# FFN1's norm weight multiplied into the input's blocks out of PSUM instead of into weight rows, and the first pair of each FFN written in another order

## The chip, the core and the metric

The kernel runs on one core of a Trainium2 chip. The metric is device microseconds of one execution, median of several runs. TensorE (PE in the profile) multiplies into PSUM, VectorE (DVE) and ScalarE (ACT) read PSUM and SBUF, GpSimd (POOL) does a few additions, and SyncE (SP) issues nearly all DMAs. Each engine takes its instructions strictly in the order in which they stand in its queue.

## What is computed

One layer with two feed-forward blocks (FFN1, FFN2) around a mixer, for 16 meta tokens, 1024 prompt tokens and 8 sample tokens, together T = 1048 columns. The change concerns the two FFNs. Cut to that:

```python
def rmsnorm(x, w):
    y = x * lax.rsqrt(jnp.mean(x * x, axis=-1, keepdims=True) + EPS)
    return y * w

def swiglu(x, wg, wu, wd):          # wg, wu: 1024 x 2816, wd: 2816 x 1024
    return (jax.nn.silu(x @ wg) * (x @ wu)) @ wd

h = h + 0.5 * swiglu(rmsnorm(h, n1), w1g, w1u, w1d)   # FFN1
...
h = h + 0.5 * swiglu(rmsnorm(h, n2), w2g, w2u, w2d)   # FFN2
```

The norm weight n1 scales the 1024 features of the input. It may be multiplied into the input or into the 1024 rows of wg and wu; the factor rsqrt(mean) of a token is applied later, to the products.

## The kernel before

**Staging.** The span begins with FFN1: 22 "pairs" (a gate and an up block of 128 columns each, `pair`), then its `down` product. The mixer follows, then FFN2 with the same 22 pairs and `down`. FFN1 reads x from memory, transposes it on PE and places it (`Input`, `first1`); FFN2 has its input on chip (`first2`).

**A pair.** The input is held as two halves of the columns, each half (c = 0, 1) as 2 x 2 blocks: features 0-511 or 512-1023 by two quarters of 262 columns. Gate and up weights of one pair are 2 x 2 blocks too (gate or up by feature half). A product of 2 x 2 by 2 x 2 blocks is made of seven block products instead of eight, so both sides need sums of blocks: `Left.sum_` (L368) makes the weights' sums, `Blocks.sum_` (L288) the input's. Every operand is split into a rounded high part (ACT, L372 for weights, L293 for the input) and the remainder (DVE, L376, L299), and a block product is 4 feature tiles by 3 matmuls (high by high, high by low, low by high; L143 to L145) of 128x262. With seven products and two halves, a pair is 14 steps of 12 matmuls. The input's operands are made once, in the first pair, and stay for all 22; the weights' are made for every pair.

**Norm weight.** In FFN1, `Left.scale` (L362) multiplies n1 into the four loaded weight tiles of a pair: 16 ACT instructions of 128x128 each, in place, ahead of the sums. In FFN2 there is no such step: the input's blocks are scaled once by `Blocks.scaled` (L282).

**What sets the order.** Both FFNs are written under a manual schedule for PE, DVE, ACT and SP: `Steps.before(i, fn)` puts fn's instructions ahead of step i, and each engine's queue follows the order in which the steps are run through. `Left.plan` gives a pair's loads, scales, sums and splits by their distance to its first step (loads 11 and 10 steps ahead, sums 7 to 5 ahead). `Hidden.jobs` puts differences of the pair's result (L542) and their stores (L545) around the pairs' ends. SP takes loads (L355) and stores in one queue. After a product, `post` takes it out of PSUM: L459 (ACT) copies product 1, L461, L466, L468, L471 and L475 (DVE) add, L454 multiplies the token factor, L464 and L473 (ACT) are the silus, L481 writes the result. Products 1 and 2, 5 and 3, 7 and 4 share a PSUM bank, so that a later product waits for the copy or the addition of the earlier one.

**First pairs.** In the first pair of each FFN the steps run half by half (here o is half 0, e is half 1), since the input arrives late. `first1` in FFN1: `Input.place` transposes x tile by tile (L843) and copies blocks out of PSUM (L849: half 0 on DVE, half 1 on ACT); `square` (L860) sums squares for the token factor; `rms` (L875) and `spread_r` (L881, L882) spread the factor over partitions; `store` (L866) writes the transposed x to memory, from where `down` reads it back. The parameters come in one tile and one transpose (`columns`, L742).

Of the kernel before, what the change touches and what calls it, by code (L numbers as in the profile page):

```python
# [262 lines left out]
class Blocks:  # L263

    def __init__(self, K, half, keep=False):
        self.K, self.half, self.keep = K, half, keep
        self.b, self.op = {}, {}
# [74 lines left out]
class Left:  # L344
# [11 lines left out]

    def scale(self, p):
        if self.wcol is not None:
            for k in range(self.n):
                c = k + (self.n if p in (4, 2) else 0)  # L360
                t = self.raw[p][:, k * P : k * P + P]
                self.K.nc.scalar.activation(t, t, AF.Identity, scale=self.wcol[:, c : c + 1])  # L362
# [73 lines left out]
def pair(K, S, wg, wu, f, ops, spread, wcol, hid, first=None):  # L436
# [8 lines left out]
    left = Left(K, [wg[:, 0:4, fs], wu[:, 0:4, fs], wu[:, 4:8, fs], wg[:, 4:8, fs]], 4, wcol)  # L445
# [239 lines left out]
def ffn(K, wg, wu, wd, ops, spread, wcol, src, first, after):  # L685
# [9 lines left out]
    with K.tc.manual_schedule(engines={E.PE, E.DVE, E.Activation, E.SP}):  # L695
        S = Steps()
        hidden = Hidden(K)
        for i in range(NF // 2):
            hid, e = [], []
            for f in (2 * i, 2 * i + 1):  # L700
                hid.append([])
                pair(K, S, wgv, wuv, f, ops, spread, wcol, hid[-1], first if f == 0 else None)
# [23 lines left out]
def parameters(K, a):  # L726

    nc = K.nc
    rows = {"norm_ffn1": 8, "norm_mix": 8, "norm_ffn2": 8, "conv_w": 32, "conv_b": 8, "hg_norm": 4, "ssm_norm": 4, "lb_logits": 8}
    off = {}  # L730
    n = 0
    prm = K.t(P)
    for name, r in rows.items():
        off[name] = (n, r)
        (nc.scalar if name == "norm_ffn1" else nc.gpsimd).dma_start(prm[n : n + r, :], a[name].rearrange("l (k p) -> (l k) p" if len(a[name].shape) == 2 else "l j (k p) -> (l j k) p", p=P))
        n += r
    K.col = K.const.tile([P, n], F32, name="col")
# [73 lines left out]
class Input:  # L811
# [23 lines left out]
    def place(self, i, copy):  # L835
# [4 lines left out]
        for b0 in range(0, KT, m):  # L840
            ps = K.psm()
            for k in range(m):
                K.nc.tensor.transpose(ps[:, k * n : k * n + n], self.x[i][:, (b0 + k) * P : (b0 + k + 1) * P], K.ident[:n, :n])  # L843
            pv = ps[:, : m * n].rearrange("p (k t) -> p k t", k=m)
            for q in range(4):
                c0, c1 = max(t0, q * Q), min(t0 + n, q * Q + Q)
                for b in range(b0 // 4, (b0 + m) // 4):
                    if c0 < c1:
                        copy(self.block(b, q)[:, :, c0 - q * Q : c1 - q * Q], pv[:, 4 * b - b0 : 4 * b - b0 + 4, c0 - t0 : c1 - t0])  # L849

    def block(self, b, q):
# [4 lines left out]
        return o.b[p].rearrange("p (k t) -> p k t", k=4)  # L856

# [614 lines left out]
def body(ctx, tc, a, o):  # L1472
# [3 lines left out]
    columns = parameters(K, a)  # L1476
    wn1, wnm, wn2 = K.pc["norm_ffn1"], K.pc["norm_mix"], K.pc["norm_ffn2"]
    hsp = K.dram.tile([D, T], F32, name="hspill")
    ops = [Blocks(K, 0, keep=True), Blocks(K, 1)]
    spread = Spread(K)  # L1480
    x = Input(K, a, ops, spread)

    def first1(S, w):
        o, e = ops
        dve, act = nc.vector.tensor_copy, nc.scalar.copy
# [7 lines left out]
        x.place(0, dve)  # L1493
        x.square(0)
        columns()
        x.place(1, dve)
        x.square(1)
        x.place(2, dve)
        w.scale(1)
        o.cast(1)  # L1500
        w.hi(1)
        o.low(1)
        x.place(3, dve)
        w.lo(1)
        x.place(4, dve)
        o.cast(2)
        w.scale(2)
        w.hi(2)
        o.low(2)
        w.lo(2)  # L1510
        o.sum_(5)
        o.cast(5)
        x.store(0)

        def before(i, *fns):
            for fn in fns:
                S.before(i, (lambda fn=fn: fn[0](*fn[1:])))

        before(1, (w.scale, 7), (w.scale, 4), (w.sum_, 5), (w.hi, 5), (o.low, 5), (w.lo, 5), (o.sum_, 6), (o.cast, 6), (x.place, 5, act), (x.square, 2))
        before(2, (w.sum_, 6), (w.hi, 6), (o.low, 6), (w.lo, 6), (o.sum_, 7), (o.cast, 7), (x.square, 3), (x.square, 4), (x.place, 6, act))  # L1520
# [217 lines left out]
```

## Time and profile before

| what | us |
|---|---|
| median of 3 runs (2224.08 to 2236.66) | 2226.96 |
| the profiled execution: its time, its span | 2225.85, 2224.1 |
| busy in the span: PE, DVE, ACT | 2044.1, 1495.2, 894.5 |
| FFN1's pairs: first gate load of pair 2 issued, that of pair 21 | 92.30, 543.48 |
| FFN2's pairs: the same two loads | 1524.86, 1916.19 |

How to read it: the page has busy times, the chain of work that ended last, and groups of instructions by line. A row of the timeline has start, duration, engine, line, operation, output and input, count, and in brackets the idle time of the engine ahead of it with what ended it. A row of waits has the engine and line that waited, what it waited for, the total in us, how often, and the longest. A row of windows has the stretch, its length, busy time of PE, PE's weight loads, DVE, ACT and POOL with counts, the granted TensorE clock, the DMA engines' busy share, and GB/s.

### The profile page before, as it was taken

How to read it: one execution, taken by the hardware profiler on the slowest of the kernel's cores; microseconds unless marked ns; L12 is line 12 of the kernel's file. 1: busy time of each engine (PE TensorE's matmuls, PEld its weight loads, DVE VectorE, ACT ScalarE, POOL GpSimd, SP SyncE). 2: the span in 40 equal slices, each digit the busy share in tenths (PEclk: the TensorE clock that was granted, in tenths of full speed). 3: DMA queues.
4: the chain of work that ended last, by engine and by line, in shares of the span. 5: the costliest groups of instructions: out<-in, count | busy, mean ns of one | idle time of the engine just before them, and what ended most of it. 6: DMA issues, size and time to landing. Idle time of an engine off the chain costs nothing.

```text
span 2224.1 us, 38759 instructions
## 1 busy us (share of the span) xinstructions
PE 2044.1 (92%) x15494; PEld 1983.2 (89%) x15494; DVE 1495.2 (67%) x2498; ACT 894.5 (40%) x1799; POOL 141.9 (6%) x175
## 2 busy tenths in 40 slices
PE   5698988998989989979999998979999999989996
PEld 4698988988989988978899997969999999989996
DVE  5666666666778767568554556576777777778863
ACT  5634434434334544365423325552222222333351
POOL 1000000000000210050110110220000000000000
PEclk8899999999999999989999999999999999999998
DMA  6133232233795551063220233322323323487651
GB/s 184 40 98 91 73 101 73 73 101 96 224 292 176 175 162 40 12 171 99 81 77 13 67 108 129 125 67 73 100 74 116 101 83 105 144 268 235 209 149 56
DMA packets 325036, 259.19 MB, mean 117 GB/s; under 512 B 17713, under 2 KB 301105, under 8 KB 324849
## 3 DMA queue, kind: packets, MB, share of 16 engines
q1 hardware_dynamic: 324616, 256.68, 38.5%
q8 instruction: 122, 2.00, 0.4%
q14 instruction: 58, 0.47, 0.1%
q0 software_dynamic: 224, 0.04, 0.0%
q10 hardware_dynamic: 16, 0.00, 0.0%
HBM read 191.26 MB, written 65.47 MB: 115 GB/s over the span
## 4 chain that ended last, share of the span: by engine, by line
PE 58%; DVE 16%; DMA 9%; ACT 7%; issue 4%; SPq 1%; POOL 1%; DVEq 0%; ACTq 0%; POOLq 0%
PE acc L143 18%; PE acc L144 17%; PE acc L145 17%; DMA r<-in_w_ffn_up_dram 5%; ACT r L362 4%; DVE t L454 2%; DVE ws L376 2%; DMA r<-in_w_ffn_down_dram 2%; PE mis L1328 1%; ACT ws L372 1%; DVE s L481 1%; DVE r L368 1%; DMA u<-hd 1%; DVE s L641 1%; DVE s L542 1%
## 5 line engine op out<-in xcount | busy, mean ns | idle before, releaser
L143 PE MATMUL acc<-u,ws 128*128 128x262 f32 (+2 forms) x4504 | 1337.3, 298 | 116.5 <-DVE t L466 53.2
L144 PE MATMUL acc<-u,ws 128*128 128x262 f32 (+2 forms) x4504 | 1326.5, 295 | 2.3 <-DVE u L299 1.2
L145 PE MATMUL acc<-u,ws 128*128 128x262 f32 (+2 forms) x4504 | 1323.9, 294 | 1.7 <-DVE ws L376 1.6
L143 PEld LDWEIGHTS acc<-u,ws 128*128 128x128 f32 x4504 | 867.5, 193 | 139.5 <-ACT r L362 46.0
L144 PEld LDWEIGHTS acc<-u,ws 128*128 128x128 f32 x4504 | 872.0, 194 | 4.6 <-DVE u L299 1.9
L145 PEld LDWEIGHTS acc<-u,ws 128*128 128x128 f32 x4504 | 868.6, 193 | 2.9 <-DVE ws L376 2.2
L376 DVE TENSOR_TENSOR ws<-r,ws 128x512 fp32r<-128x512 f32 x308 | 212.2, 689 | 162.9 <-ACT ws L372 162.9
L372 ACT CAST ws<-r 128x512 fp32r<-128x512 f32 x308 | 175.0, 613 | 5.9 <-PE acc L145 5.1
L362 ACT ACTIVATE r<-r,col 128x128 f32<-128x128 f32 x352 | 108.0, 388 | 119.5 <-DMA r<-in_w_ffn_up_dram 119.5
L368 DVE TENSOR_TENSOR r<-r,r 128x512 f32<-128x512 f32 x176 | 119.3, 697 | 29.2 <-ACT r L362 24.0
L473 ACT ACTIVATE t<-t 128x524 f32<-128x524 f32 (+1 forms) x46 | 28.7, 623 | 269.2 <-DVE t L454 269.2
L204 POOL TENSOR_TENSOR t<-t,t 128x262 f32<-128x262 f32 x56 | 52.0, 943 | 886.4 <-ACT t L203 886.4
L641 DVE SCALAR_TENSOR_TENSOR s<-acc,s 128x524 f32<-128x524 f32 (+1 forms) x120 | 77.4, 662 | 43.8 <-PE acc L145 42.7
L570 DVE TENSOR_TENSOR u<-u,u 128x1048 fp32r<-128x1048 f32 (+1 forms) x84 | 97.0, 1159 | 8.4 <-ACT u L566 8.0
L454 DVE TENSOR_TENSOR t<-t,u 128x524 f32<-128x524 f32 (+1 forms) x138 | 93.9, 680 | 4.6
L618 ACT CAST ws<-r 128x512 fp32r<-128x512 f32 (+1 forms) x84 | 47.8, 582 | 107.4 <-DVE r L613 38.0
L618 ACT CAST ws<-u 128x512 fp32r<-128x512 f32 (+1 forms) x72 | 42.1, 585 | 114.0 <-DVE u L613 107.2
L138 DVE TENSOR_TENSOR ws<-r,ws 128x512 fp32r<-128x512 f32 x88 | 60.3, 697 | 40.7 <-ACT ws L137 40.6
L623 DVE TENSOR_TENSOR ws<-r,ws 128x512 fp32r<-128x512 f32 (+1 forms) x84 | 56.9, 691 | 41.3 <-ACT ws L618 41.3
L566 ACT CAST u<-u 128x1048 fp32r<-128x1048 f32 (+1 forms) x84 | 83.2, 992 | 1.5 <-DMA u<-hd 1.4
L137 ACT CAST ws<-r 128x512 fp32r<-128x512 f32 x88 | 53.9, 617 | 72.8 <-PE acc L145 52.0
L464 ACT ACTIVATE t<-t 128x524 f32<-128x524 f32 (+1 forms) x46 | 28.3, 616 | 119.2 <-DVE t L454 119.2
(355 smaller groups left out, 1957.6 us busy)
## 6 DMA issues: line engine op xcount, KB each, us to landing
hd<-s SPq DMA_DIRECT2D x170, 262.0 KB
r<-in_w_ffn_down_dram SPq DMA_DIRECT2D x128, 256.0 KB
u<-hd SPq DMA_DIRECT2D x56, 524.0 KB
r<-in_w_ffn_gate_dram SPq DMA_DIRECT2D x88, 256.0 KB
r<-in_w_ffn_up_dram SPq DMA_DIRECT2D x88, 256.0 KB
r<-in_w_in_dram SPq DMA_DIRECT2D x56, 256.0 KB
r<-in_w_ffn_down_dram SPq DMA_DIRECT2D x64, 192.0 KB
u<-hd SPq DMA_DIRECT2D x28, 393.0 KB
```

The source lines that it names most:

```text
L143: mm(ps, whi, xhi, start=first, stop=False, skip_group_check=more)
L144: mm(ps, whi, xlo, start=False, stop=False, skip_group_check=more)
L145: mm(ps, wlo, xhi, start=False, stop=last, skip_group_check=more)
L362: self.K.nc.scalar.activation(t, t, AF.Identity, scale=self.wcol[:, c : c + 1])
L368: self.K.nc.vector.tensor_tensor(self.raw[p], self.raw[x], self.raw[y], op)
L372: self.K.nc.scalar.copy(self.w[p][:, : self.n * P], self.raw[p])
L376: self.K.nc.vector.tensor_sub(t[:, 512 : 512 + w], self.raw[p], t[:, :w].bitcast(F32))
L454: nc.vector.tensor_mul(t, t if src is None else src, spread.lanes(i, cs))
L566: K.nc.scalar.copy(hi, lo.bitcast(F32))
L570: K.nc.vector.tensor_sub(lo, lo.bitcast(F32), hi.bitcast(F32))
L618: nc.scalar.copy(w[p, j, g][:, : n * P], src)
L641: nc.vector.scalar_tensor_tensor(t, b, 0.5, t, ALU.mult, ALU.add)
```

## The change

Norm weight: `Left.scale` is gone, and so are its places in `plan`; a pair's loads stand one step later (10 and 9 steps ahead instead of 11 and 10), in both FFNs. Instead `Input.place` writes each piece out of PSUM twice: scaled by n1 into the block that the products use (on DVE with n1 broadcast along the tokens), and unscaled into a block of its own for the store (on ACT). Half 1 is transposed by feature tile instead of by token tile (`place_k`), so that ACT can scale by a column. n1's column gets its own small transpose (`columns1`), ahead of the other parameters'. The lists of `first1` and `first2` are written in another order, and `post_first` takes product 2 with product 3 instead of with product 7.

```diff
 class Left:
-    def scale(self, p):
-        if self.wcol is not None:
-            for k in range(self.n):
-                c = k + (self.n if p in (4, 2) else 0)
-                t = self.raw[p][:, k * P : k * P + P]
-                self.K.nc.scalar.activation(t, t, AF.Identity, scale=self.wcol[:, c : c + 1])
...
-            ((1, 7, 4, 2), (-11, -11, -10, -10), self.load),
-            ((7, 4, 1, 2), (-9, -8, -8, -7), self.scale),
+            ((1, 7, 4, 2), (-10, -10, -9, -9), self.load),
             ((5, 6, 7, 3), (-7, -7, -6, -5), self.sum_),
...
         elif p == 7:
             nc.vector.tensor_add(temp("u1", cs), b, temp("x", cs))
+        elif p == 3:
             post(2, cs, late[2])
+            post(3, cs, b)
             times_r("u1", 1, cs)
...
 class Input:
+        def scaled(b):
+            for q, cs, src in parts(b):
+                w = self.wcol[:, 4 * b : 4 * b + 4, None].broadcast_to([P, 4, cs.stop - cs.start])
+                K.nc.vector.tensor_tensor(self.block(b, q)[:, :, cs], src, w, ALU.mult)
+
+        def raw(b):
+            for q, cs, src in parts(b):
+                K.nc.scalar.copy(self.raw_block(b, q)[:, :, cs], src)
...
+    def place_k(self, k):
+        K = self.K
+        ps = K.psm()
+        for i in range(4):
+            K.nc.tensor.transpose(ps[:, i * P : i * P + P], self.x[5 + i][:, k * P : k * P + P], K.ident)
+        for q, c0, c1 in ((2, 0, Q), (3, Q, 4 * P)):
+            K.nc.scalar.activation(self.block(k // 4, q)[:, k % 4, : c1 - c0], ps[:, c0:c1], AF.Identity, scale=self.wcol[:, k : k + 1])
+            K.nc.scalar.copy(self.raw_block(k // 4, q)[:, k % 4, : c1 - c0], ps[:, c0:c1])
...
 first1
-        before(4, (x.spread_r, 0), (w.sum_, 3), (w.hi, 3), (o.low, 3), (w.lo, 3), (o.sum_, 4), (o.cast, 4), (x.place, 8, act), (x.place, 9, act), (x.store, 1))
-        before(5, (e.cast, 1), (e.low, 1), (e.cast, 2), (e.sum_, 5), (e.low, 2), (e.cast, 5), (x.square, 5))
...
+        before(S, 4, (o.low, 3), (w.lo, 3), (tail,), (e.cast, 1), (e.sum_, 5), (o.cast, 4), (x.place_k, 4), (x.rms, 0), (x.place_k, 5))
+        before(S, 5, (x.spread_r, 0), (o.low, 4), (e.cast, 5), (e.low, 1), (x.place_k, 6), (x.place_k, 7), (x.store, 1))
+        before(S, 6, (e.cast, 2), (e.sum_, 6), (e.low, 5), (e.cast, 6), (e.low, 2), (x.square, 5), (x.square, 6))
...
 first2
-        for p in (1, 5, 2, 6, 7, 3):
-            w.split(p)
+        w.split(1)
+        w.split(5)
         e.scaled(h, wn2, (1, 7))
...
+        w.split(2)
         e.low(5)
+        w.split(6)
         e.scaled(h, wn2, (2, 3))
```

**A pair of FFN1 on SP.** What stands in SP's queue around the loads of pair 3, before: three stores of the result before it (hd, from tiles s), the four loads of the pair (gate and up, first feature half, then up and gate, second half), and more stores.

```order
L545 DMA hd_112<-s_943 256x1x262
L545 DMA hd_109<-s_943 256x1x262
L545 DMA hd_108<-s_712 256x1x262
L355 DMA r_998<-in_w_ffn_gate_dram 128x4x128
L355 DMA r_1000<-in_w_ffn_up_dram 128x4x128
L355 DMA r_1019<-in_w_ffn_up_dram 128x4x128
L355 DMA r_1021<-in_w_ffn_gate_dram 128x4x128
L545 DMA hd_111<-s_996 256x1x262
L545 DMA hd_113<-s_996 256x1x262
```

The same place with the change (names are numbered anew, lines moved by a few):

```order
L538 DMA hd_113<-s_942 256x1x262
L538 DMA hd_110<-s_942 256x1x262
L538 DMA hd_109<-s_727 256x1x262
L354 DMA r_1014<-in_w_ffn_gate_dram 128x4x128
L354 DMA r_1016<-in_w_ffn_up_dram 128x4x128
L538 DMA hd_112<-s_995 256x1x262
L354 DMA r_1032<-in_w_ffn_up_dram 128x4x128
L354 DMA r_1034<-in_w_ffn_gate_dram 128x4x128
L538 DMA hd_114<-s_995 256x1x262
```

One store now stands between the first two and the last two loads. It is so in every second pair (those with odd numbers), in both FFNs; in the others the order of SP is as before.

**The first pair of FFN1 on ACT**, from the casts of half 1's first blocks (u) to the copy of half 1's product 1, before:

```order
L293 CAST u_469<-u_284 128x1048
L293 CAST u_473<-u_291 128x1048
L293 CAST u_479<-u_475 128x1048
L860 ACTIVATE s_133,st_102<-s_133 128x1024
L362 ACTIVATE r_382<-r_382,col 128x128 x4
L473 ACTIVATE t_498<-t_498 128x262
L293 CAST u_506<-u_504 128x1048
L860 ACTIVATE s_135,st_102<-s_135 128x1024
L860 ACTIVATE s_137,st_102<-s_137 128x1024
L362 ACTIVATE r_446<-r_446,col 128x128 x4
L362 ACTIVATE r_380<-r_380,col 128x128 x4
L459 COPY t_258<-acc_245 128x262
```

With the change, from the last pieces of `place_k` to the same copy:

```order
L871 COPY u_407<-mis_489 128x250
L455 ACT_TABLE_LOAD
L455 ACTIVATE t_518<-t_518 128x262
L464 ACTIVATE t_521<-t_521 128x262
L292 CAST u_526<-u_420 128x1048
L292 CAST u_532<-u_528 128x1048
L887 ACTIVATE s_134,st_103<-s_134 128x1024
L887 ACTIVATE s_136,st_103<-s_136 128x1024
L450 COPY t_275<-acc_374 128x262
```

The scales of pair 1's weights are gone from here, one square fewer stands ahead of the copy, and two casts of half 1 went ahead of the silus.

**The first pair of FFN2 on ACT**, from the first casts of half 1 to the copy of half 0's product 1, before:

```order
L293 CAST u_14882<-u_14872 128x1048
L293 CAST u_14888<-u_14884 128x1048
L282 ACTIVATE u_14892<-s_13598,col 128x262
L282 ACTIVATE u_14892<-s_13600,col 128x262
L282 ACTIVATE u_14892<-s_13602,col 128x262
L282 ACTIVATE u_14892<-s_13604,col 128x262
L282 ACTIVATE u_14897<-s_13598,col 128x262
L282 ACTIVATE u_14897<-s_13600,col 128x262
L282 ACTIVATE u_14897<-s_13602,col 128x262
L282 ACTIVATE u_14897<-s_13604,col 128x262
L459 COPY t_14914<-acc_14758 128x262
```

With the change, ahead of the same copy (L203 are the squares of the out projection's last results, s):

```order
L203 ACTIVATE t_14450<-s_13299 128x262
L281 ACTIVATE u_14581<-s_13299,col 128x262
L281 ACTIVATE u_14586<-s_13293,col 128x262
L203 ACTIVATE t_14467<-s_13299 128x262
L281 ACTIVATE u_14586<-s_13295,col 128x262
L281 ACTIVATE u_14586<-s_13297,col 128x262
L281 ACTIVATE u_14586<-s_13299,col 128x262
L364 CAST ws_14591<-r_14481 128x512
L364 CAST ws_14594<-r_14547 128x512
L450 COPY t_14609<-acc_14453 128x262
```

The first casts of half 1 and most of its scaled pieces now stand further ahead, among the squares of the out projection; three pieces and two weight casts are left between the last square and the copy.

More of the change, by code (lines that the diff above doesn't have):

```diff
@@ L263, with __init__ @@
 class Blocks:
[L267 to L268 removed]
+    def __init__(self, K, half):
+        self.K, self.half = K, half
         self.b, self.op = {}, {}
@@ L286, in sum_ @@
         x, y = self.b[x], self.b[y]
-        t = self.b[p] if p == 7 and not self.keep else self.new(p)
+        t = self.b[p] if p == 7 else self.new(p)
         self.K.nc.vector.tensor_sub(t, x, y)
@@ L433, in halves, with pair @@
     return t.rearrange("p (c t) -> p c t", c=2)
-def pair(K, S, wg, wu, f, ops, spread, wcol, hid, first=None):
+def pair(K, S, wg, wu, f, ops, spread, hid, first=None):
     nc = K.nc
@@ L701, in ffn @@
                 hid.append([])
-                pair(K, S, wgv, wuv, f, ops, spread, wcol, hid[-1], first if f == 0 else None)
+                pair(K, S, wgv, wuv, f, ops, spread, hid[-1], first if f == 0 else None)
                 e.append(len(S.steps))
@@ L833, in load, with place @@
                     self.K.nc.sync.dma_start(self.x[i][r0 - t0 : r1 - t0], src[r0 - p0 : r1 - p0])
-    def place(self, i, copy):
+    def place(self, i):
         K = self.K
@@ L1492, in first1 @@
         nc.scalar.preload_act_table_set("sqrt_and_others")
-        x.place(0, dve)
-        x.square(0)
[L1495 to L1517, printed above, removed]
@@ L1519, in first1 @@
-        before(1, (w.scale, 7), (w.scale, 4), (w.sum_, 5), (w.hi, 5), (o.low, 5), (w.lo, 5), (o.sum_, 6), (o.cast, 6), (x.place, 5, act), (x.square, 2))
-        before(2, (w.sum_, 6), (w.hi, 6), (o.low, 6), (w.lo, 6), (o.sum_, 7), (o.cast, 7), (x.square, 3), (x.square, 4), (x.place, 6, act))
-        before(3, (w.sum_, 7), (w.hi, 7), (o.low, 7), (w.lo, 7), (x.rms, 0), (o.cast, 3), (x.place, 7, act))
-        before(4, (x.spread_r, 0), (w.sum_, 3), (w.hi, 3), (o.low, 3), (w.lo, 3), (o.sum_, 4), (o.cast, 4), (x.place, 8, act), (x.place, 9, act), (x.store, 1))
@@ L1523, in first1 @@
-        before(5, (e.cast, 1), (e.low, 1), (e.cast, 2), (e.sum_, 5), (e.low, 2), (e.cast, 5), (x.square, 5))
-        before(6, (e.low, 5), (e.sum_, 6), (e.cast, 6), (o.low, 4), (x.square, 6), (x.square, 7))
-        before(7, (e.low, 6), (e.sum_, 7), (e.cast, 7), (x.square, 8), (x.square, 9))
-        before(8, (x.rms, 1), (w.split, 4), (e.low, 7), (e.sum_, 4), (e.cast, 3))
-        before(9, (e.low, 3), (e.cast, 4))
-        before(10, (x.spread_r, 1), (e.low, 4))
+        columns1()
+        for i in range(2):
+            scaled, raw = x.place(i)
+            for fn in (scaled, raw):
+                fn(0)
+                fn(1)
@@ new lines, in first1 @@
+        w.hi(1)
+        scaled, raw2 = x.place(2)
+        scaled(0)
+        o.cast(1)
+        scaled(1)
+        raw2(0)
+        raw2(1)
+        scaled, raw3 = x.place(3)
+        scaled(0)
+        o.low(1)
+        scaled(1)
+        w.lo(1)
+        w.hi(2)
+        o.cast(2)
+        scaled, raw4 = x.place(4)
+        scaled(0)
+        scaled(1)
+        raw3(0)
+        raw3(1)
+        o.low(2)
+        o.sum_(5)
+        w.lo(2)
+        o.cast(5)
+        w.sum_(5)
+        w.hi(5)
@@ new lines, in first1, with tail @@
+        raw4(0)
+        raw4(1)
+        x.store(0)
+        columns()
+        o.sum_(6)
+        x.square(0)
+        def tail():
+            scaled, raw = x.place(9)
+            for fn in (scaled, raw):
+                fn(0)
+                fn(1)
+        before(S, 1, (o.low, 5), (w.lo, 5), (o.cast, 6), (w.sum_, 6), (w.hi, 6), (o.sum_, 7), (x.square, 1))
+        before(S, 2, (o.low, 6), (w.lo, 6), (o.cast, 7), (w.sum_, 7), (w.hi, 7), (w.sum_, 3), (o.sum_, 4), (x.place_k, 0), (x.place_k, 1), (x.square, 2))
@@ L1529, in first1 @@
+        before(S, 7, (e.sum_, 7), (e.low, 6), (e.cast, 7), (e.sum_, 4), (x.square, 7), (x.square, 8), (x.square, 9))
+        before(S, 8, (w.hi, 4), (e.low, 7), (w.lo, 4), (e.cast, 3), (x.rms, 1))
+        before(S, 9, (e.cast, 4), (e.low, 3))
+        before(S, 10, (x.spread_r, 1), (e.low, 4))
         return 1, 2, 5, 6, 7, 3, 4
```

93 lines of the change are left out of this document (53 added, 40 removed).

## Prediction

> **What bounds the kernel now.** I read the page first (the span, the chain that ended last, the groups), then the same stage of both FFNs side by side.
>
> ```profile
> span 2224.1 us, 38759 instructions
> ...
> L362 ACT ACTIVATE r<-r,col 128x128 f32<-128x128 f32 x352 | 108.0, 388 | 119.5 <-DMA r<-in_w_ffn_up_dram 119.5
> ```
>
> The execution took 2225.85, 1.75 above its span and 1.1 below the median shown (2226.96); I count against 2225.85. L362, the norm weight on FFN1's weight tiles, costs ACT 108 us, and ACT sat idle 119.5 us ahead of it until a load landed. Idle time costs only where PE waits for it, so I compare stretches: the third and fifth number of a row are the length and PE's busy time. The second row is FFN1 from the load of pair 2 to that of pair 21, the fourth is FFN2 between the same loads, the third FFN2's first pair.
>
> ```profile
> 0.00:92.30 92.30, 52.88 (x295) 46.70 (x296) 55.14 (x94) 56.96 (x117) 10.13 (x34) 0.82 0.40 120
> 92.30:543.48 451.18, 408.20 (x3200) 404.70 (x3199) 296.22 (x457) 193.76 (x495) 0.00 (x0) 0.96 0.29 84
> 1478.00:1524.86 46.86, 32.60 (x211) 31.47 (x212) 32.03 (x52) 24.84 (x45) 1.62 (x2) 0.85 0.07 24
> 1524.86:1916.19 391.33, 390.64 (x3199) 390.12 (x3198) 294.47 (x457) 104.58 (x191) 0.00 (x0) 1.00 0.33 97
> ```
>
> 3200 matmuls, 457 DVE instructions and the same loads take 451.18 us in FFN1 and 391.33 in FFN2, over 19 periods each: 23.75 and 20.60 us a pair. In FFN2 PE is busy for all but 0.69 us, at full granted clock (1.00). FFN1 differs by 304 ACT instructions (495 less 191), which are 19 times the 16 scales. The waits of the two stretches, FFN1's three first:
>
> ```profile
> ACT r L362 <- DMA r<-in_w_ffn_up_dram: 114.4, 20, 7.9
> PEld acc L143 <- ACT r L362: 44.6, 18, 4.2
> PE acc L143 <- DVE t L466: 43.0, 19, 4.0
> ...
> DVE r L368 <- DMA r<-in_w_ffn_up_dram: 4.3, 5, 1.4
> PE acc L143 <- DVE t L466: 0.7, 2, 0.4
> ```
>
> In FFN1 PE waits 19 times for L466 (43.0 us in all), in FFN2 twice (0.7). One pair of FFN1 shows how:
>
> ```profile
> 143.71 1.28 ACT L362 ACTIVATE r<-r,col 128x128 f32<-128x128 f32 x4 [5.69 <-DMA r<-in_w_ffn_up_dram]
> ...
> 145.94 3.61 ACT L362 ACTIVATE r<-r,col 128x128 f32<-128x128 f32 x12
> ...
> 149.03 0.70 DVE L466 TENSOR_TENSOR t<-acc,t 128x524 f32<-128x524 f32 x1
> ...
> 149.87 0.40 PE L143 MATMUL acc<-u,ws 128*128 128x262 f32 x1 [1.86 <-DVE t L466]
> ```
>
> ACT stands at the load, then scales; the silu and the casts behind the scales come late; DVE stands at the sums, which need scaled tiles; the PSUM addition L466 is queued behind the sums, and PE needs its bank. The scale also holds ACT while the load is under way.
>
> **Term 1, the scales of pairs 1 to 21: -61.3 us.** I take FFN2's pairs as what FFN1's become, between marks that both have: the copy of pair 1's product 1 and the last result of pair 21.
>
> ```profile
> 90.89 0.60 ACT L459 COPY t<-acc 128x524 f32<-128x524 f32 x1 [3.40 <-PE acc L145]
> ...
> 587.82 1.32 DVE L481 TENSOR_TENSOR s<-t,t 128x524 f32<-128x524 f32 x2
> ...
> 1523.27 0.60 ACT L459 COPY t<-acc 128x524 f32<-128x524 f32 x1 [3.49 <-PE acc L145]
> ...
> 1958.92 1.32 DVE L481 TENSOR_TENSOR s<-t,t 128x524 f32<-128x524 f32 x2
> ```
>
> FFN1: 587.82 - 90.89 = 496.9. FFN2: 1958.92 - 1523.27 = 435.65. Difference 61.3. Past this nothing is left to win there: PE is late next, and it is full.
>
> **Term 2, the loads one step later, behind a store: +10 us.** In every odd pair a store of 262 KB now stands between the first two and the last two loads. The first sum needs the second up load, the third of the four. FFN2 shows how much room there is:
>
> ```profile
> 1604.12 1.32 DVE L481 TENSOR_TENSOR s<-t,t 128x524 f32<-128x524 f32 x2
> 1624.62 1.32 DVE L481 TENSOR_TENSOR s<-t,t 128x524 f32<-128x524 f32 x2
> 1635.62 1.42 DVE L368 TENSOR_TENSOR r<-r,r 128x512 f32<-128x512 f32 x2 [1.38 <-DMA r<-in_w_ffn_up_dram]
> 1646.05 1.32 DVE L481 TENSOR_TENSOR s<-t,t 128x524 f32<-128x524 f32 x2
> 1666.14 1.32 DVE L481 TENSOR_TENSOR s<-t,t 128x524 f32<-128x524 f32 x2
> ...
> 1626.00:1636.00 10.00, 10.00 (x84) 10.00 (x84) 6.08 (x10) 3.60 (x7) 0.00 (x0) 1.00 0.82 238
> ```
>
> An undisturbed pair takes 20.50 (1624.62 - 1604.12). The two after it, with a DVE wait of 1.38 at the load, take 41.52 instead of 41.00: PE loses the wait less 0.86. At the 238 GB/s of that burst 262 KB are 1.10 us. If the load lands that much later, the five odd pairs that wait now (4.3 us) wait 9.8, and PE loses 9.8 - 5 x 0.86 = 5.5, of which about 1 is lost already; the five that do not wait lose at most 1.10 - 0.86 = 0.24 each. That is 4.5 to 5.7 an FFN; I take 5, twice. Ends: 0, if the store only shares the burst that it follows today, and +43: at the stage's mean of 97 GB/s the load is 2.7 later, 5 x 2.7 + 4.3 - 4.3 = 13.5 and 5 x 1.84 = 9.2, less 1, per FFN. What DVE holds up while it stands at the sum is L466, and PE behind it. The nearer row is the burst's own.
>
> The Trainium skill speaks against this place: "DMA: Bandwidth & Descriptors", section "Queues, rings and completion order", says that an issuing engine's DMAs share one ring per DMA engine, taken in ring order, so that bytes ahead in SP's queue are paid before the load. By that rule the term is the +10; if transfers shared the rate evenly it would be near 0.
>
> **Term 3, FFN1's first pair: -8 us.** PE is busy for 52.88 of its 92.30 us, at a clock of 0.82. Two of its longest waits, and ACT ahead of the second:
>
> ```profile
> 43.79 1.68 PE L881 MATMUL mis<-t,ones 128*128 128x262 f32 x3 [6.47 <-ACT t L875]
> ...
> 46.14 0.67 ACT L882 COPY u<-mis 128x262 f32<-128x262 f32 x2
> ...
> 31.37 1.07 ACT L849 COPY u<-mis 128x512 f32<-128x512 f32 x2
> ...
> 58.67 1.26 ACT L362 ACTIVATE r<-r,col 128x128 f32<-128x128 f32 x4
> ...
> 64.00 2.43 ACT L362 ACTIVATE r<-r,col 128x128 f32<-128x128 f32 x8
> 66.33 0.35 ACT L459 COPY t<-acc 128x262 f32<-128x262 f32 x1
> ...
> 66.74 0.58 PE L143 MATMUL acc<-u,ws 128*128 128x262 f32 x1 [9.61 <-ACT t L459]
> ```
>
> ACT is what PE waits for. Removed from ACT here: 32 scales (pairs 0 and 1) at 2.33 / 8 = 0.29, 9.3 us, and half 1's copies (six of 128x512 at 0.53, six pieces at about 0.3), 5 us. Added: half 0's unscaled copies, the same 5 us, and for half 1 32 pieces of about 128x262 at 0.33, 10.6, with 0.6 for the last tile: 16.2. ACT's work so stays about equal (+2), and DVE's scaled copies take the place of its plain ones, one for one. What changes is the order: ahead of the copy L459 12 scales (3.5), one square (1.2) and two casts (2) are gone, 6.7 of the 9.61 us. The 6.47 is ACT's token factor, which stays on ACT's path and is now behind `place_k`'s pieces. Ends: -16.1, both waits gone; +6, if nothing is saved and half 1's extra 5.6 us on ACT delay it all. Scaling an ACT copy and multiplying out of PSUM on DVE are not shown at these shapes; the ends hold them. I take -8, near the 6.7, with a little for n1's own early transpose, which no longer holds PE ahead of the second tile.
>
> **Term 4, FFN2's first pair: -6 us.**
>
> ```profile
> 1484.54 3.33 ACT L282 ACTIVATE u<-s,col 128x262 f32<-128x262 f32 x8
> 1487.78 0.36 ACT L459 COPY t<-acc 128x262 f32<-128x262 f32 x1
> ...
> 1488.19 0.59 PE L143 MATMUL acc<-u,ws 128*128 128x262 f32 x1 [5.09 <-ACT t L459]
> ...
> 1499.74 0.59 PE L143 MATMUL acc<-u,ws 128*128 128x262 f32 x1 [5.43 <-DVE t L466]
> ```
>
> PE waits 5.09 us for a copy out of PSUM that ACT has queued behind eight scaled pieces, 0.41 each. With the change three pieces and two weight casts stand between the last square of the out projection and that copy, 2.3 us: the 5.09 go. The 5.43 behind it is DVE's, and one low part fewer (1.2) stands ahead of L466. What moved ahead stands among the out projection's squares, where ACT waits for DVE anyhow; it may still delay them. Ends: 0 (the wait only moves), and both waits with the clock: 32.60 us busy at 0.85 would be 4.9 shorter at 1.00, together -15.4.
>
> The Trainium skill, "TensorE: Matmul & The Clock Gate", section on the HAM clock gate, halves the clock after an idle window of about 3.4 us; the 0.85 beside two waits of over 5 us agrees. By it the term would be nearer -9, since both cold starts cost extra; I leave that to the end of the range.
>
> **Sum:** -61.3 + 10 - 8 - 6 = -65.3; 2225.85 - 65.3 = 2160.5. I forecast **2160**.
>
> **Rivals.**
>
> *Slower: the store holds the loads.* Place: SP's queue in the 20 odd pairs. The rest wins 61.3 + 8 + 6 = 75.3, so it turns the sign from 3.8 us of PE per odd pair, a load some 4.2 us later, which for 262 KB is 62 GB/s. Against it: 238 in the burst. A little beyond: 2240. Chance 0.02. At the mean of 97 GB/s it is the +43: 2194, chance 0.08.
>
> *The first pairs give nothing*: +6 and 0 instead of -8 and -6. For it: ACT's work there does not shrink, and pair 1's last two loads stand behind four stores of half 1. 2225.85 - 61.3 + 10 + 6 = 2180.5. Chance 0.15.
>
> *More is won*: the store costs nothing and every wait named in the first pairs goes: 2225.85 - 61.3 - 16.1 - 15.4 = 2133. Chance 0.15, mostly short of that end.
>
> *The scale is gone and its stall is not*: DVE waits for the loads instead. FFN2 has the same loads and waits 4.3 us in 19 pairs. If half the 61.3 stayed: 2191. Chance 0.03.
>
> **How the numbers follow.** My forecast, 2148 to 2173, has 0.57. Range 2140 to 2180: it takes in most of the first pairs' ends and half of the store's. A measurement of this kernel tells about 0.5% (11 us) from no change; all cases but the slower one lie below 2216: faster 0.96, same 0.02, slower 0.02.
>
> **What would show it.** Right: a period of 20.5 to 21.2 us in FFN1's pairs, PE busy throughout at clock 1.00, L466 hardly waited for; DVE's wait at the load near 10 us in each FFN, all in odd pairs; FFN1's pair 1 copy (90.89 now) near 83; FFN2's first pair with one wait over 5 us less. Wrong: if FFN1's pairs stay above 22 us, the stall was the load's; if DVE's wait at the load does not grow, the store costs nothing; if a first pair is as long as now with other waits, its order only moved them.

## The result, and the profile after

The changed kernel takes **2144.75 us** (median of 4 runs, 2139.6 to 2148.69) against 2227.97 for the kernel before beside it: a ratio of 0.962, 95% interval 0.9585 to 0.9655. The forecast was 2160, the range 2140 to 2180. The profiled execution has a span of 2143.3 us, 80.8 less than before.

The same marks as in the prediction cut the span into stretches. First the page's span, then the timeline of the changed kernel at the copy of pair 1 (now L450) and the last result of pair 21 (now L472), in FFN1 and in FFN2, and between them PE's matmul in the out projection that waits 1.65 us for a sum:

```profile
span 2143.3 us, 38415 instructions
```

```profile
75.43 0.60 ACT L450 COPY t<-acc 128x524 f32<-128x524 f32 x1 [3.45 <-PE acc L145]
...
512.29 1.32 DVE L472 TENSOR_TENSOR s<-t,t 128x524 f32<-128x524 f32 x2
...
1388.37 0.39 PE L143 MATMUL acc<-u,ws 128*128 128x262 f32 x1 [1.65 <-DVE s L1472]
...
1440.87 0.60 ACT L450 COPY t<-acc 128x524 f32<-128x524 f32 x1 [3.11 <-PE acc L145]
...
1877.96 1.32 DVE L472 TENSOR_TENSOR s<-t,t 128x524 f32<-128x524 f32 x2
```

Of the kernel before, four of these marks stand in the prediction. The fifth, the wait in the out projection, is:

```profile
1461.27 0.39 PE L143 MATMUL acc<-u,ws 128*128 128x262 f32 x1 [1.64 <-DVE s L1445]
```

| stretch | before | after | difference | predicted |
|---|---|---|---|---|
| start to the copy of pair 1 in FFN1 | 90.89 | 75.43 | -15.5 | -8 (term 3) |
| FFN1, copy of pair 1 to last result of pair 21 | 496.93 | 436.86 | -60.1 | -61.3 + 5 (terms 1 and 2) |
| from there to the out projection's wait (not touched) | 873.45 | 876.08 | +2.6 | 0 |
| from there to the copy of pair 1 in FFN2 | 62.00 | 52.50 | -9.5 | -6 (term 4) |
| FFN2, copy of pair 1 to last result of pair 21 | 435.65 | 437.09 | +1.4 | +5 (term 2) |
| rest | 265.2 | 265.3 | +0.2 | 0 |

The differences add up to -80.9, the 80.8 of the spans but for rounding; the prediction had -65.3. Each stretch is read from one profile, and the same code differs from one profile to the next: in five profiles whose first pair of FFN1 is the changed one, the copy of pair 1 comes at 73.55 to 75.43, and in six profiles with FFN2's first pair as before, its stretch takes 60.5 to 63.1. Three views show how it looks inside. The windows over the first pairs of before (FFN1's, then the stretch with FFN2's) and of after, with the pairs of both FFNs; the third number is the length, the fourth PE's busy time (not the fifth, as the prediction has it), and the granted clock stands behind POOL's count:

```profile
0.00:90.89 90.89, 51.47 (x283) 45.28 (x284) 54.10 (x92) 55.55 (x114) 10.13 (x34) 0.81 0.40 119
1461.27:1523.27 62.00, 46.86 (x318) 44.73 (x319) 40.68 (x67) 30.27 (x57) 10.04 (x12) 0.89 0.14 48
```

```profile
75.43:512.29 436.86, 433.01 (x3546) 430.94 (x3545) 328.08 (x505) 122.81 (x220) 0.00 (x0) 1.00 0.36 107
1440.87:1877.96 437.09, 433.56 (x3545) 432.57 (x3544) 328.25 (x505) 122.83 (x220) 0.00 (x0) 1.00 0.36 107
0.00:75.43 75.43, 48.25 (x284) 44.87 (x285) 53.76 (x95) 56.20 (x117) 10.14 (x34) 0.84 0.48 144
...
1388.37:1440.87 52.50, 43.36 (x318) 41.77 (x319) 40.79 (x67) 29.99 (x57) 10.99 (x12) 0.93 0.17 57
```

The two FFNs now run alike, 436.86 and 437.09, PE busy for all but some 4 us at full clock: what a pair of FFN1 lost is gone. In the first pairs, read busy and idle apart. FFN1's: 39.4 us idle before (90.89 less 51.47 busy), 27.2 after; busy 3.2 less, at a better clock. FFN2's: idle 15.1 and 9.1, busy 3.5 less.

The waits of the changed kernel over the pairs, FFN1's stretch, then FFN2's (total, times, longest):

```profile
DVE r L360 <- DMA r<-in_w_ffn_up_dram: 14.3, 13, 2.1
...
PE acc L143 <- DVE t L457: 2.2, 3, 1.1
...
DVE r L360 <- DMA r<-in_w_ffn_up_dram: 10.4, 13, 2.0
```

The stall on the PSUM addition (L466 before, L457 now) went from 44.3 us between these marks (43.0 in the prediction's window) to 2.2. In its place stands DVE at the up load, 10.4 us in FFN2, as large as forecast ("near 10"), and 14.3 in FFN1. But PE hardly pays for it.

### The profile page after: what moved, and what is told of

It reads as the page before. It is cut to its first block, busy times and chain, and to the rows that moved or that the text cites. A ratio compares the mean times of both kernels' runs of the same rounds, so it can differ in the third digit from the quotient of the medians.

```text
span 2143.3 us, 38415 instructions
## 1 busy us (share of the span) xinstructions
PE 2022.2 (94%) x15495; PEld 1966.2 (92%) x15495; DVE 1494.5 (70%) x2501; ACT 801.0 (37%) x1481; POOL 141.1 (7%) x175
## 4 chain that ended last, share of the span: by engine, by line
PE 45%; DVE 5%; DMA 3%; ACT 1%; issue 1%; SPq 0%; POOL 0%; DVEq 0%; ACTq 0%; POOLq 0%
PE acc L143 13%; PE acc L144 13%; PE acc L145 13%; PE mis L1355 2%; DMA r<-in_w_ffn_down_dram 1%; DMA u<-hd 1%; DMA r<-in_w_ffn_up_dram 1%; DVE s L634 1%; PE mis L1394 0%; PE mis L1450 0%; PE mis L1412 0%; DVE s L1357 0%; PE mis L1431 0%; PE mis L1334 0%; DVE s L1369 0%
## 5 line engine op out<-in xcount | busy, mean ns | idle before, releaser
L445 DVE TENSOR_TENSOR t<-t,u 128x524 f32<-128x524 f32 (+1 forms) x138 | 93.5, 680 | 4.7
L445 DVE TENSOR_TENSOR t<-acc,u 128x524 f32<-128x524 f32 (+1 forms) x46 | 31.2, 679 | 60.5 <-PE acc L145 60.5
```

The lines of the kernel that those rows point to most:

```text
L445: nc.vector.tensor_mul(t, t if src is None else src, spread.lanes(i, cs))
```

## The experiments

All times are beside runs of the kernel before on the same chip; ratios are to it. Where a few microseconds matter I compare stretches between marks.

**The scales away, their wait alone, their work alone.** Three versions of the kernel before. The first skips the scales:

```diff
     def scale(self, p):
-        if self.wcol is not None:
+        if False:
```

> The kernel before without FFN1's 352 scales (the norm weight n1 is left out of the computation), nothing else changed. Theory (term 1 as predicted, and the scales hold only the copy L459 in the first pair): FFN1 from the copy of pair 1 to the last result of pair 21 goes from 496.9 to 435.7 us, the first pair shrinks by 3 to 5 us, nothing else moves: about 2161 us. Rival (the stall is the load's, not the scales'): DVE waits for the loads in ACT's place, the stretch stays above 465 us and the time above 2190. Rival for the first pair (its gain is all the scales' work on ACT, not the order): the first pair shrinks by 9 to 15 us, about 2152.

The second leaves ACT one column per load, the third replaces the scales by work that waits for nothing:

```diff
-            for k in range(self.n):
...
-                self.K.nc.scalar.activation(t, t, AF.Identity, scale=self.wcol[:, c : c + 1])
+            self.K.nc.scalar.copy(self.K.scr, self.raw[p][:, 0:1])
```

> The kernel before with every group of four scales replaced by one ACT copy of a single column of the loaded tile into a scratch column (n1 is left out of the computation): ACT still stands in its row until each load has landed, but does next to no work there. Theory (it takes both: the scales' 4.9 us a pair come after the load, so everything behind them is late): the wait alone leaves the stretch of pairs 1 to 21 below 450 us (435.7 without any of it, 496.9 now). Rival (ACT standing at the load is what costs): above 465 us.

```diff
-                self.K.nc.scalar.activation(t, t, AF.Identity, scale=self.wcol[:, c : c + 1])
+                self.K.nc.scalar.activation(self.K.scr, self.K.ident, AF.Identity, scale=self.wcol[:, c : c + 1])
```

> The kernel before with every scale replaced by an ACT activation of the same size at the same place that reads the constant identity and writes a scratch tile (n1 is left out of the computation): the work stays on ACT, the wait for the load goes. Theory (it takes both): the stretch of pairs 1 to 21 is below 450 us. Rival (the 108 us of ACT work are what costs, wherever they stand): above 465 us. The first pair keeps its scales' work, so it should stay as in the kernel before, at 88 to 91 us to the copy of pair 1.

That third version wrote a bf16 scratch tile, and its instructions kept ACT busy for 0.402 us each, where the scales took 4.9 us for 16, 0.31 each. So its stretch of 469.1, above the 465 of the rival, is not that of the same work. Its copy of pair 1 came at 92.61, a little above the 88 to 91 expected. A fourth keeps shape and types, with a factor of 1 in place of the column:

```diff
-                self.K.nc.scalar.activation(t, t, AF.Identity, scale=self.wcol[:, c : c + 1])
+                if self.in_plan:
+                    self.K.nc.scalar.activation(self.K.ident, self.K.ident, AF.Identity, scale=1.0)
...
```

> The kernel before with the scales of pairs 1 to 21 replaced by ACT activations of the same shape and types that multiply the constant identity by 1 in place (n1 is left out of those pairs; pair 0 keeps its scales): the work of 4.9 us a pair as it was (the scratch version's took 0.43 us each instead of 0.31, 6.9 us a pair), without the wait for the load. Theory (work and wait together make the stall): the stretch of pairs 1 to 21 below 450 us. Rival (ACT's work costs by itself, in proportion to its length): 434.3 + 34.8 x 4.9 / 6.9 = 459 us or more.

The groups by line of the third and fourth (busy, mean ns), then ACT's wait at the up load in the second, all three from 92 to 510 us:

```profile
L362 ACT ACTIVATE scr<-ident,col 128x128 bf16<-128x128 f32 x304 | 122.2, 402 | 8.6
```

```profile
L363 ACT ACTIVATE ident<-ident 128x128 f32<-128x128 f32 x320 | 99.3, 310 | 8.8
```

```profile
ACT scr L359 <- DMA r<-in_w_ffn_up_dram: 107.7, 28, 6.5
```

| version | wait on ACT | ACT work a pair | stretch of pairs 1 to 21 | all, ratio (95%) |
|---|---|---|---|---|
| scales left out | no | 0 | 434.28 | 0.9724 (0.9703-0.9744) |
| wait alone | yes | 4 copies of one column | 436.35 | 0.9728 (0.9701-0.9755) |
| work alone | no | 16 x 0.310 = 5.0 | 448.0 | 0.9816 (0.9785-0.9847) |
| longer work alone | no | 16 x 0.402 = 6.4 | 469.1 | 0.9919 (0.989-0.9948) |
| kernel before | yes | 4.9 | 496.93 | 1 |

Left out, the scales give 62.6 us in this stretch (61.3 forecast). ACT standing at the loads, 118.0 us over the whole stretch, costs 2.1. The work alone costs 13.7. Together they cost 62.6, so 46.8 of it only comes when the work stands behind the load: it starts when the load has landed, and the silu, the casts and DVE's sums stand behind it. How much of the 46.8 goes which way is not shown. In the kernel before, DVE's sums also need the scaled tiles (DVE waits 19.0 us for them in this stretch). In none of the three versions that take wait and work apart do the sums need ACT's result, and no version has wait and work without that dependence. The theory's bound of 450 held for the equal work by 2 us only. Between the two versions with work alone, 1.5 us more work a pair (16 x 0.092) cost 1.0 more a pair (21.1 / 21): there two thirds of the added work went into the pair's length. In the first pair the scales were worth 7.3 us (copy of pair 1 at 83.63 instead of 90.89), more than the theory's 3 to 5 and less than its rival's 9.

**The loads one step later, without the rest.**

```diff
-            ((1, 7, 4, 2), (-11, -11, -10, -10), self.load),
+            ((1, 7, 4, 2), (-10, -10, -9, -9), self.load),
```

> The kernel before with the four weight loads of each pair one step (1.46 us) later, as the change has them, and the scales kept. Theory (in FFN1 all that stands behind the scales follows the load): each of 21 pairs of FFN1 is 1 to 1.5 us longer, 20 to 31 us, and FFN2 1.4 us longer as in the changed kernel: 2247 to 2260. Rival (the store does not delay the loads, and a step has slack in FFN1): within 5 us of the kernel before. In FFN2, DVE's wait at the up load should grow from 4.3 to about 10 us.

A ratio of 1.0023 (1.0001 to 1.0045), medians 5.7 us apart, just outside the rival's 5; FFN1's stretch, in one profile each, 5.7 us shorter, not 20 to 31 longer: the theory fell. SP's queue shows why. Timeline of before and of this version at one odd pair, DVE's result, then SP:

```profile
206.56 1.32 DVE L481 TENSOR_TENSOR s<-t,t 128x524 f32<-128x524 f32 x2
...
207.91 1.85 SPq L545 DMA_DIRECT2D hd<-s  x3
209.86 0.57 SPq L355 DMA_DIRECT2D r<-in_w_ffn_gate_dram  x1
210.52 1.21 SPq L355 DMA_DIRECT2D r<-in_w_ffn_up_dram  x2
```

```profile
205.25 1.32 DVE L481 TENSOR_TENSOR s<-t,t 128x524 f32<-128x524 f32 x2
...
206.59 1.86 SPq L545 DMA_DIRECT2D hd<-s  x3
208.55 0.56 SPq L355 DMA_DIRECT2D r<-in_w_ffn_gate_dram  x1
209.21 0.55 SPq L355 DMA_DIRECT2D r<-in_w_ffn_up_dram  x1
209.85 0.59 SPq L545 DMA_DIRECT2D hd<-s  x1
210.53 0.56 SPq L355 DMA_DIRECT2D r<-in_w_ffn_up_dram  x1
```

In both the first load is issued 1.98 us after the end of L481, behind three stores, the first of which is issued as that result ends. In the other odd pairs of FFN1 the first load comes 1.97 to 2.00 us behind that result in both versions. The step never set the load's time there, the stores ahead of it do. What "one step later" adds is the fourth store: the second up load is issued 1.98 us after the first load instead of about 1.3. In FFN2 DVE's wait rose to 9.0 us, near the 10 expected.

**The loads of the changed kernel one step earlier, and all four behind the store.**

```diff
-            ((1, 7, 4, 2), (-10, -10, -9, -9), self.load),
+            ((1, 7, 4, 2), (-11, -11, -10, -10), self.load),
```

> The changed kernel with the four weight loads of each pair back where the kernel before had them (one step earlier, all four ahead of the store). Theory after the first look (the store's price is what exceeds DVE's slack of 0.86 us in each wait: 3.3 us in FFN1 and 2.5 less 1.1 in FFN2): 2 to 5 us faster than the changed kernel, about 2141. Prediction's term 2: 10 us faster, 2135. Rival (two stores ahead of a burst delay as much as one inside it): the same within 1 us.

The other version has (-9, -9, -9, -9):

> The changed kernel with all four weight loads of a pair at the later of the two steps, so that all four stand behind the store. Theory (each load lands later by up to 1.46 us, DVE has 0.86 us of slack): waits of DVE at the up load rise from 10 to 14 us an FFN to 25 to 40, and PE loses what exceeds the slack, 10 to 25 us in all: 2155 to 2170. Rival (the bytes ahead of the second up load are the same, only the first two loads move): within 3 us of the changed kernel.

DVE's wait at the up load, FFN1 and FFN2, with the loads early:

```profile
DVE r L360 <- DMA r<-in_w_ffn_up_dram: 7.7, 11, 1.7
...
DVE r L360 <- DMA r<-in_w_ffn_up_dram: 4.1, 6, 1.8
```

and with all behind the store:

```profile
DVE r L360 <- DMA r<-in_w_ffn_up_dram: 11.2, 11, 2.0
...
DVE r L360 <- DMA r<-in_w_ffn_up_dram: 11.3, 12, 1.7
```

Early, the stretches are 434.00 and 435.33, together 4.6 us less than changed, as the theory has it and less than half of what the prediction's term 2 had (medians 2141.2 and 2144.75; ratio 0.9616, 0.9592 to 0.9641, which the totals cannot tell from 0.962). Late, they are 436.58 and 438.20, 0.8 more in all, ratio 0.9648 (0.9628 to 0.9669): here the theory fell and the rival held. The waits follow the store ahead of the second up load, not the step: 7.7, 14.3 and 11.2 us in FFN1, 4.1, 10.4 and 11.3 in FFN2. The Trainium skill, "DMA: Bandwidth & Descriptors", section "Queues, rings and completion order", states that on each DMA engine descriptors are consumed in ring order. The waits agree in direction, with the store ahead of the load; that its bytes are paid in full they do not show, as the part on term 2 works out.

**FFN1's first pair in the old order.** In the changed kernel the lists of `first1` are put back as before, as far as they go; what needs no scale stays out:

```diff
-        before(S, 2, (o.low, 6), (w.lo, 6), (o.cast, 7), (w.sum_, 7), (w.hi, 7), (w.sum_, 3), (o.sum_, 4), (x.place_k, 0), (x.place_k, 1), (x.square, 2))
+        before(S, 2, (w.sum_, 6), (w.hi, 6), (o.low, 6), (w.lo, 6), (o.sum_, 7), (o.cast, 7), (x.square, 3), (x.square, 4), (x.place_k, 2), (x.place_k, 3))
...
```

> The changed kernel with FFN1's first pair written in the order of the kernel before as far as it goes: every tile's scaled and unscaled copies at once, squares, casts and low parts where they stood, two feature tiles of half 1 where a token tile stood, both parameter transposes ahead of the first tile; the scales stay out. Theory (the gain of 15.5 us is the order's): the copy of pair 1 comes at 86 to 92 us instead of 75.4, 2156 to 2162. Rival (the gain is the scales' work that has left ACT): 75 to 79 us, 2145 to 2149.

> As the version of the changed kernel with FFN1's first pair in the order of before, but with the larger parameter transpose behind the first tile, where the kernel before has it (there it stood ahead of the first tile, and PE waited 8.2 us for a parameter's load). Theory (the order of the later steps is what is worth most): the copy of pair 1 at 88 to 93 us, 4 to 7 us earlier than 95.6. Rival (the transposes' place was most of it): below 84 us.

The copy of pair 1 came at 95.60 in the first and 93.45 in the second (ratios 0.9719, 0.9698 to 0.974, and 0.9729, 0.9698 to 0.9761), 3.6 and 0.5 us above what the theory gave, far from the rivals. The second differs from the first by 2.2 us, about what the same code differs by from profile to profile. It doesn't price the transposes' place in full: PE still waits 5.16 us there for a parameter's load, and not at all in the changed kernel, where that transpose comes later. So the order as a whole is worth 18.0 us (93.45 to 75.43), the transposes' place included. PE's long waits, the second version's timeline, then the changed kernel's:

```profile
12.29 0.35 PE L739 MATMUL mis<-ident,t 72*128 72x72 f32 x1 [5.16 <-DMA t<-in_lb_logits_dram]
...
47.56 2.11 PE L908 MATMUL mis<-t,ones 128*128 128x262 f32 x4 [9.36 <-ACT t L902]
...
70.40 0.59 PE L143 MATMUL acc<-u,ws 128*128 128x262 f32 x1 [6.86 <-ACT t L450]
```

```profile
21.25 0.59 PE L143 MATMUL acc<-u,ws 128*128 128x262 f32 x1 [4.44 <-ACT t L450]
...
42.05 2.12 PE L908 MATMUL mis<-t,ones 128*128 128x262 f32 x4 [4.52 <-ACT t L902]
...
54.60 0.59 PE L143 MATMUL acc<-u,ws 128*128 128x262 f32 x1 [4.97 <-ACT t L450]
```

ACT has as many instructions in both (117; 57.05 and 56.20 us busy up to the mark). What differs is what is queued ahead of the ones PE waits for. Of the 18.0 us, 13.7 are PE's idle time and 4.4 its busy time. Beside it stands the kernel before without scales, copy of pair 1 at 83.63: taking the scales away gave 7.3, the multiplication out of PSUM and the unscaled copies on ACT, in the old order as far as it goes, cost 9.8, the new order gave 18.0; sum -15.5.

**FFN2's first pair, list and post-processing apart.** The first version has the old list of `first2` (all six weight splits ahead of half 1's scaled blocks), the second the new list but product 2 finished at product 7 as before:

```diff
             nc.vector.tensor_add(temp("u1", cs), b, temp("x", cs))
-        elif p == 3:
+            if order[1] == 5:
+                post(2, cs, late[2])
+                times_r("u1", 1, cs)
+        elif p == 3 and order[1] != 5:
```

> The changed kernel with FFN2's first pair written in the order of the kernel before (six weight splits ahead of the second half's scaled blocks). Theory (term 4: the 5.1 us wait for the copy out of PSUM comes back): 5 to 7 us slower, about 2151. Rival (the rest between the FFNs gave the 6.9 us, or the gain is from the post-processing of products 2 and 3 taken together): within 2 us.

> The changed kernel with the post-processing of product 2 in FFN2's first pair back at product 7, as before, and the rest as changed. From the out projection's wait of 1.65 us for the sum of the residual to the copy of pair 1 the changed kernel takes 52.5 us, with the old list 57.4, before 62.0. Theory (taking 2 and 3 together gives the 4.6 us that the list does not): about 57 us, 4 to 5 us slower in all. Rival (the list gives all, and the rest lies in the out projection): 52 to 53 us and no change in the time.

Windows from the out projection's wait to the copy of pair 1, of the one and of the other:

```profile
1386.63:1444.03 57.40, 44.69 (x318) 42.59 (x319) 40.51 (x67) 30.39 (x58) 9.97 (x12) 0.91 0.15 52
```

```profile
1394.94:1448.30 53.36, 43.43 (x318) 41.82 (x319) 40.94 (x67) 29.79 (x58) 10.98 (x12) 0.94 0.16 56
```

| from the wait to the copy | post as before | post as changed |
|---|---|---|
| list as before | 62.00 | 57.40 |
| list as changed | 53.36 | 52.50 |

The old list costs 4.9 us on top of the new post-processing, a little under the theory's 5 to 7, and its wait for the copy is back (timeline of the version with the old list):

```profile
1413.60 0.58 PE L143 MATMUL acc<-u,ws 128*128 128x262 f32 x1 [5.10 <-ACT t L450]
```

The theory on the post-processing fell: beside the new list it gives 0.9, beside the old one 4.6. The 62.00 is the kernel before itself, which has its loads a step earlier too and took 60.5 to 63.1 in six profiles, so the 4.6 is rougher than the others. The two shorten the same stretch, and the list is the larger part. The totals (0.9659, 0.9637 to 0.9681, and 0.9662, 0.9635 to 0.9688) do not separate these two.

**A version meant to beat both.** Early loads, squares and a cast moved behind the copies that PE waits for, and the norm's end in FFN2 two steps later:

```diff
...
-        before(S, 2, (e.low, 2), (e.cast, 6), (e.sum_, 7), (nf2.end, 2), (nf2.end, 3, False))
+        before(S, 2, (e.low, 2), (e.cast, 6), (e.sum_, 7))
...
-        before(S, 4, (e.low, 7), (e.cast, 3))
+        before(S, 4, (e.low, 7), (e.cast, 3), (nf2.end, 2), (nf2.end, 3, False))
```

> The changed kernel with three edits: weight loads back one step earlier; in FFN1's first pair two squares each moved behind the copy out of PSUM that PE waits for, with product 5's cast and the last unscaled copies behind it too; in FFN2's first pair the norm's end two steps later, so that DVE's chain for it no longer stands ahead of the addition that PE waits 6.4 us for. Theory: loads 3 to 5 us, FFN1's first pair 2 to 4 us (copy of pair 1 at 71 to 73 instead of 75.4), FFN2's first pair 3 to 5 us (52.5 to about 48): 8 to 14 us faster than the changed kernel, 2131 to 2137. Rival (the waits only move to what is late next): as the version with the early loads alone, 2141.

It didn't: 0.9647 (0.962 to 0.9673), median 2145.35. The pairs of both FFNs kept the gain of the early loads (434.57 and 434.77); the first pairs gained nothing. The windows from half 1's copy to the copy of pair 1 in FFN1, of the changed kernel and of this version:

```profile
54.20:75.43 21.23, 17.63 (x114) 17.11 (x115) 17.84 (x35) 14.16 (x28) 0.00 (x0) 0.84 0.07 21
```

```profile
51.54:75.86 24.32, 18.87 (x114) 18.27 (x115) 19.24 (x36) 16.26 (x31) 0.00 (x0) 0.79 0.05 18
```

Two of PE's waits in FFN2's first pair, then its window:

```profile
1415.96 0.39 PE L143 MATMUL acc<-u,ws 128*128 128x262 f32 x1 [1.71 <-DVE t L457]
...
1423.24 0.56 PE L143 MATMUL acc<-u,ws 128*128 128x262 f32 x1 [5.55 <-DVE t L445]
```

```profile
1387.12:1440.61 53.49, 42.91 (x319) 41.13 (x320) 40.79 (x67) 30.13 (x58) 10.99 (x12) 0.94 0.16 56
```

In FFN1 the wait of 4.44 at the first copy is down to 0.47 and half 1's copy comes 2.7 us earlier (51.54), yet the copy of pair 1 comes at 75.86. The last stretch is 3.1 us longer: 1.8 of it is the wait for the token factor, 5.03 instead of 3.20, behind the squares that were moved; 1.2 is busy time, at a granted clock of 0.79 instead of 0.84. Over the whole first pair PE is idle 2.0 us less (25.2) and busy 2.4 us more (50.69). In FFN2 the wait for L457 fell from 6.37 to 1.71, and 5.55 for L445, which multiplies that late norm in, took its place: 53.49 instead of 52.50. The rival held: the waits moved, and the version is no faster than the one with the early loads alone.

## Why the prediction came out as it did

**Term 1 was right**, size and mechanism: -62.6 with the scales alone away, against -61.3. What the prediction only argued, that ACT's waiting and its work together make the stall, is now shown: neither alone makes a quarter of it. How much of it goes through DVE's sums, which needed the scaled tiles, stays open.

**Term 2 had its mechanism in part and was mis-sized**: +2.6 in FFN1 (436.86 against the 434.28 without scales and with the loads early) and +1.4 in FFN2, where it had 5 each. Five profiles have the changed order of the loads: 435.7 to 437.75 in FFN1, 434.6 to 437.3 in FFN2. With the early order three profiles take 434.0 to 434.6 in FFN1, seven 434.75 to 435.7 in FFN2. So FFN1's loss is clear; in FFN2 the means differ by 1.0 and the ranges overlap.

What failed is the step that made the load 1.10 us later, the time of the store's bytes, in the five pairs that waited already. Those five wait 6.1 us now (2.04, 0.40, 1.17, 0.66, 1.80), not 9.8; before it was 4.3 (1.38, 0.47, 1.32, 0.17, 0.98). The other five odd pairs wait 3.1 and three even pairs 1.2. That this adds up to 10.4, near the forecast's 10, is luck, and "all in odd pairs" was wrong. Why the store's price is so much below 1.10 us was not found. The slack of 0.86 held in the pairs shown here. These are three of the four waits of after that exceed it in FFN2 (the fourth is 0.90), and the results (L472) at both ends of the two pairs around the first:

```profile
1542.22 1.32 DVE L472 TENSOR_TENSOR s<-t,t 128x524 f32<-128x524 f32 x2
1553.87 1.42 DVE L360 TENSOR_TENSOR r<-r,r 128x512 f32<-128x512 f32 x2 [2.04 <-DMA r<-in_w_ffn_up_dram]
...
1584.49 1.32 DVE L472 TENSOR_TENSOR s<-t,t 128x524 f32<-128x524 f32 x2
...
1677.40 1.42 DVE L360 TENSOR_TENSOR r<-r,r 128x512 f32<-128x512 f32 x2 [1.17 <-DMA r<-in_w_ffn_up_dram]
...
1801.39 1.42 DVE L360 TENSOR_TENSOR r<-r,r 128x512 f32<-128x512 f32 x2 [1.80 <-DMA r<-in_w_ffn_up_dram]
```

The wait of 2.04 made its two pairs 42.27 instead of 41.00: 1.27, where 2.04 less 0.86 gives 1.18. Over the slack the four lie by 1.18 + 0.04 + 0.31 + 0.94 = 2.5 us. Before, the waits of 1.38, 1.32 and 0.98 lay over it by 1.1. The difference, 1.4, is what the stretch lost. In FFN1 3.3 lie over the slack now and 0.9 without the scales; the stretches differ by 2.6. Other profiles of the same code stray from this rule by up to 1.5 us a stretch. Nine of the thirteen waits in FFN2 are shorter than the slack and free.

**Term 3 came out inside its ends, but not in the place that it priced**: -15.5 against -8. The step that failed is the choice near "6.7 of the 9.61". The wait that it priced fell by 4.6 (to 4.97), but at the copy of half 0, where PE waited 0.6 us before, it now waits 4.44. PE's waits in this pair, two of before and one of after:

```profile
PE acc L143 <- ACT t L459: 10.2, 2, 9.6
...
PE mis L742 <- DMA r<-in_w_ffn_gate_dram: 3.7, 1, 3.7
```

```profile
PE acc L143 <- ACT t L450: 9.4, 2, 5.0
```

In sum PE waits for these copies nearly as long as before, and for the token factor too (7.5 before, 7.7 after). The 12.2 us of idle time went elsewhere: 6.4 of waiting for DVE (its PSUM addition and low parts, 7.2 before, 0.8 after), 3.7 of waiting for a load at the parameters' transpose, and about 2 in small waits for ACT. The prediction had DVE's work as one for one and gave the transpose "a little". The busy time fell by 3.2. That the order wins was right; that it won more than 8 is luck as far as the term's own account goes. The new order was worth 18 us, the operations cost net 2.5.

**Term 4** forecast 6 us of idle time, and idle fell by 6.0 (15.1 to 9.1): the 5.09 went, and the wait for DVE's addition grew from 5.43 to 6.37, where the prediction had one low part fewer ahead of it. The 3.5 of busy time beside it, left to the end of the range, made it -9.5. The prediction's sentence on the Trainium skill's "TensorE: Matmul & The Clock Gate", section on the HAM clock gate, put the term near -9; the -9.5 agrees, with a granted clock of 0.93 where it was 0.89.

**The rivals.** The store holding the loads did not come near 3.8 us a pair; the first pairs gave more, not nothing; the stall did not stay. The time lies between the forecast and "more is won", the range's low side: the two halves of term 2 and terms 3 and 4 all missed in the same direction, by 3.8, 3.6, 7.5 and 3.5 us (the first with term 1's 61.3 in it). 2.6 us the other way come from the stretch that the change does not touch.

## What to carry to other kernels

An engine that stands idle at a load costs next to nothing by itself (2.1 us here); work put behind that wait, ahead of what others need, costs much of its length in every pair (3.0 of 4.9 us), and the same stage elsewhere in the program, without that work, prices it best. A step in a schedule is a place in a queue, not a time: look for what stands ahead of a moved DMA on its engine and what that waits for. A wait only counts for what exceeds the slack behind it, pair by pair, and a first stage full of waits is priced by its idle and busy time together, since the long waits looked at here are followed by slow matmuls. Moving work from one wait to the next gains nothing if it makes that next wait longer.

## What the runs showed of the hardware

A long wait is paid beyond its length. Timeline of the changed kernel in FFN2's first pair:

```profile
1421.06 0.58 PE L143 MATMUL acc<-u,ws 128*128 128x262 f32 x1 [6.37 <-DVE t L457]
1421.44 0.42 PE L144 MATMUL acc<-u,ws 128*128 128x262 f32 x1
1421.66 0.42 PE L145 MATMUL acc<-u,ws 128*128 128x262 f32 x1
...
1428.15 0.29 PE L145 MATMUL acc<-u,ws 128*128 128x262 f32 x1
1428.27 0.29 PE L143 MATMUL acc<-u,ws 128*128 128x262 f32 x1
```

Behind the wait the matmuls start 0.22 us apart, later 0.12. At that rate the 24 of two products take 5.3 us instead of 2.9, so by this estimate the 6.37 us of waiting cost over 2 more in busy time. The 3.2 and 3.5 us less of busy time in the first pairs, with about the same number of matmuls and a better granted clock, fit that. But less idle time alone does not bring it: the version meant to beat both is idle 25.2 us in FFN1's first pair, the changed kernel 27.2, and it is busy 50.69 us, where five profiles of the changed first pair have 47.35 to 48.25.

And the stretch from FFN1's last pair result to the out projection, the same code in all these kernels, took between 871.3 and 882.0 us from one profile to the next. What makes these 10 us was not found; a difference of a few microseconds between two spans says nothing here until the stretches are compared.
